# Two softmax attentions with heads in pairs on half the array each, and weights kept in rows padded with zeros

## The chip, the cores and the metric

The kernel runs on one core of one Trainium2 chip, in one launch. The metric is the device time of that launch in microseconds. A core has five engines that work beside each other and wait for one another by semaphores: PE (the 128x128 matrix array), DVE (vector), ACT (scalar), POOL, and SP, which here only issues DMAs. PE writes to PSUM; DVE and ACT empty it.

## The reference, cut to what matters

A model of three attention layers on 256 tokens with 16 more in front (272 keys): a mixer with two attentions (`stick_breaking`, and `dsa_attention`, a softmax over the keys that an index picks), a mixture of 32 experts, a retention layer, and an attention with latent keys and values (MLA), the second softmax. All in f32, width 1024. The parts that the change touches:

```
def dsa_attention(q_full, kv_all, q_idx, w_idx, k_idx, pos, topk):       # 8 heads, key width 16 + 128
        s_idx = relu(einsum('bqhd,bkd->bqhk', qi, k_idx))                 # index heads of width 64
        score = einsum('bqh,bqhk->bqk', wi, s_idx);  _, sel = top_k(masked score, topk)      # topk 64
        logits = einsum('bqhc,bqkc->bqhk', qf, kv_sel) * scale
        p = softmax(where(valid, logits, -1e30))
        return einsum('bqhk,bqkc->bqhc', p, kv_sel[..., ROPE_DIM:])
def mla_mixer(...):                                                       # 8 heads, key width 128 + 64
        sc = einsum('bqhd,bkhd->bhqk', q[:, s:e], k[:, :e])               # query blocks of 128
        p = softmax(where(mask, sc, MASK_VALUE));  outs.append(einsum('bhqk,bkhd->bqhd', p, v[:, :e]))
```

A query of the first block of 128 sees the keys 0 to 143 only, one of the second block all 272.

## The kernel before

Everything but the attentions is dense matmuls of streamed weights: `Stream.next` cuts a weight block into a high and a low part (L285 on ACT, L286 on DVE), `tiles` issues three matmuls for each 128x128 block (L298 to L300), moving 256 or 272 columns. `dense` makes one output tile of it, in two halves, and between them calls `step`, which advances every generator in `self.gens` by one `yield`. The attentions are such generators, so each of their steps stands in the middle of a dense tile on PE. A planner of the language then moves instructions of each engine somewhat against the order of the code, by its own costs. DMAs are all on the SP queue, in order.

The pieces that the change touches:

- `index` in `mixer` (L579 to L602): scores of 8 index heads of width 64 against one key head, for both query blocks (144 and 272 keys), one head per step; ReLU on ACT (L589), weighted sum on DVE (L591); then eight steps of top-k on DVE (L597, L598), which leave the mask `msk`.
- `latent` in `mixer` (L548 to L573): the keys `kf` and the values `vb` from the latent. The values of the keys 128 to 143 and 256 to 271 go as two 16-row pieces to rows 0 to 15 and 32 to 47 of the third block of `vb`.
- `sparse` in `mixer` (L697 to L721): the first softmax attention, ten steps. Step n issues the scores of head n (per query block: the mask added by a bf16 matmul, L718, and then a matmul over the 64 rows of the head, L719) and `weigh`; then `turned` of head n - 1; and, at odd heads, the `mix` of the two heads before.
- `weigh` (L1440): softmax of one head's 128 x 416 scores (two query blocks side by side, 144 + 272): two maxima and their scaling on DVE (L1448, L1449), two exponentials on ACT (L1451), the reciprocal and two scalings on DVE (L1452, L1454).
- `turned` (L1457): the weights transposed on PE: three 128x128 pieces (L1464 to L1466) and two of 16 rows (L1467; L1468, a plain matmul with the identity, in two passes), then copies (L1470 on ACT, L1473 and L1474 on DVE, to `rest`).
- `mix` (L1477): three matmuls per head (L1480 to L1482), the middle one over the 48 rows of `rest`.
- `turn` and `attention` in `latent` of the second model (L1373 to L1407): the same for the last attention, two heads per generator, key width 128 (L1393) plus 64 (L1394), and values transposed in two full and two 16-row pieces (L1379, L1380).

`stick`, the first layer's other attention, is untouched. It already takes its heads in pairs: the two heads' matmuls of 64 rows stand next to each other, one on rows 0 to 63 and one on rows 64 to 127 (L651), and its mix writes columns 0 to 63 and 64 to 127 (L685).

An f32 matmul is two passes (two weight loads and two matmuls) in the profile; transposes, bf16 and the dense f32r matmuls are one.

Behind the first mixer, the memory of its attentions is given back (`early.close()`), and the loads of expert weights into `raw2` (L1027, on SP) wait for that.

## Time and profile before

| | |
|---|---|
| median of 3 runs | 1544.19 us (1543.4 to 1546.91) |
| the profiled execution | 1543.42 us |
| its span, first to last instruction | 1541.6 us |
| mean granted clock of PE | 0.918 |
| PE busy | 1368.4 us (89%), 9784 instructions |
| PE weight loads | 1067.3 us (69%) |
| DVE busy | 738.2 us (48%) |
| ACT busy | 532.5 us (35%) |
| POOL busy | 131.8 us (9%) |

A shape such as 64*128 64x144 is the used part of the array (rows*columns) and the moving operand. In timelines an instruction's length is from its start to the end of its result, and neighbours on PE overlap; how much time one takes from PE is read from the next one's start. A row with x4 merges four instructions of one line.

### The profile page before, as it was taken

The numbers are of one execution on the slowest core, as the hardware profiler recorded it, in microseconds if no ns is written. First come the engines' busy times: TensorE is split into PE (matmuls) and PEld (weight loads), VectorE is DVE, ScalarE is ACT, GpSimd is POOL, SyncE is SP. The second block draws the span as 40 slices with busy tenths as digits, with TensorE's granted clock in tenths as the row PEclk, the third lists the DMA queues.
The fourth block names the chain that finished last, engine by engine and source line by source line (L and its number), as shares of the span: only waits on it lengthen the run. The fifth ranks groups of instructions, "written<-read, shape, count | busy, mean of one in ns | idle before, by whom it ended". The sixth has DMA issues, their size and how long they took to land.

```text
span 1541.6 us, 23923 instructions
## 1 busy us (share of the span) xinstructions
PE 1368.4 (89%) x9784; PEld 1067.3 (69%) x9784; DVE 738.2 (48%) x1464; ACT 532.5 (35%) x928; POOL 131.8 (9%) x146
## 2 busy tenths in 40 slices
PE   8999998776676767666999999999999999999997
PEld 7898796221111212113999999999999877899997
DVE  7676566110100101003766665766567755666654
ACT  5465443100000000004233443544445443454442
POOL 4010021000000000002121211100011201100001
PEclk9999998976868768777999999999999999999998
DMA  8433386999999999997434344455545423355551
GB/s 300 124 124 97 110 286 260 420 419 371 421 420 420 421 420 421 421 421 318 153 114 148 133 141 154 154 175 169 187 164 180 160 87 108 111 169 189 189 179 71
DMA packets 55267, 359.56 MB, mean 233 GB/s; under 512 B 6384, under 2 KB 7024, under 8 KB 15600
## 3 DMA queue, kind: packets, MB, share of 16 engines
q1 hardware_dynamic: 55152, 357.97, 61.5%
q8 instruction: 79, 1.29, 0.3%
q14 instruction: 36, 0.29, 0.1%
HBM read 356.90 MB, written 1.05 MB: 232 GB/s over the span
## 4 chain that ended last, share of the span: by engine, by line
PE 49%; DVE 2%; ACT 1%; issue 0%; POOL 0%; DVEq 0%; ACTq 0%; POOLq 0%
PE acc L298 14%; PE acc L300 14%; PE acc L299 14%; DVE wl L286 1%; PE att L383 1%; ACT wh L285 1%; PE att L1394 1%; PE att L414 1%; PE att L1295 0%; PE att L1271 0%; DVE U L290 0%; PE att L1393 0%; PE att L1297 0%; PE att L1285 0%; PE att L1296 0%
## 5 line engine op out<-in xcount | busy, mean ns | idle before, releaser
L298 PE MATMUL acc<-U,wh 128*128 128x272 f32 (+1 forms) x1456 | 426.1, 293 | 12.0 <-ACT U L289 7.0
L299 PE MATMUL acc<-U,wl 128*128 128x272 f32 (+1 forms) x1456 | 418.9, 288 | 2.0 <-DVE wl L286 2.0
L300 PE MATMUL acc<-U,wh 128*128 128x272 f32 (+1 forms) x1456 | 419.1, 288 | 0.0
L286 DVE TENSOR_TENSOR wl<-raw,wh 128x1024 fp32r<-128x1024 f32 x232 | 285.9, 1232 | 155.8 <-ACT wh L285 155.3
L285 ACT ACTIVATE wh<-raw 128x1024 fp32r<-128x1024 f32 x232 | 245.6, 1060 | 319.2 <-PE acc L300 214.0
L298 PEld LDWEIGHTS acc<-U,wh 128*128 128x128 f32 x1456 | 277.9, 191 | 20.7 <-issue 8.2
L299 PEld LDWEIGHTS acc<-U,wl 128*128 128x128 f32 x1456 | 277.1, 190 | 2.6 <-DVE wl L286 2.4
L300 PEld LDWEIGHTS acc<-U,wh 128*128 128x128 f32 x1456 | 276.9, 190 | 0.4
L974 PE MATMUL acc<-raw,U 128*32 128x512 f32 x1024 | 190.4, 837 | 91.1 <-DMA raw<-in_wm 87.1
L974 PEld LDWEIGHTS acc<-raw,U 128*32 128x32 f32 x1024 | 24.6, 125 | 240.3 <-DMA raw<-in_wm 216.4
L985 DVE TENSOR_TENSOR hid<-hid,acc 128x512 f32<-128x512 f32 x8 | 5.5, 688 | 262.5 <-PE acc L974 262.5
L300 PE MATMUL acc<-hl,wh 128*128 128x272 f32 (+1 forms) x352 | 100.1, 284 | 0.0
L299 PE MATMUL acc<-hh,wl 128*128 128x272 f32 (+1 forms) x352 | 99.8, 284 | 0.0
L298 PE MATMUL acc<-hh,wh 128*128 128x272 f32 (+1 forms) x352 | 99.8, 284 | 0.0
L286 DVE TENSOR_TENSOR wl<-rawh,wh 128x512 fp32r<-128x512 f32 x112 | 80.6, 731 | 26.5 <-ACT wh L285 26.4
L1000 PE MATMUL att<-raw,ht 128*32 128x512 f32 x512 | 73.6, 690 | 19.3 <-DMA raw<-in_wm 15.6
L285 ACT ACTIVATE wh<-rawh 128x512 fp32r<-128x512 f32 x112 | 68.1, 626 | 46.8 <-PE acc L300 33.1
L1009 DVE TENSOR_TENSOR h<-h,att 128x512 f32<-128x512 f32 x32 | 22.0, 688 | 118.4 <-PE att L1007 118.4
L298 PEld LDWEIGHTS acc<-hh,wh 128*128 128x128 f32 x352 | 66.4, 189 | 0.0
L300 PEld LDWEIGHTS acc<-hl,wh 128*128 128x128 f32 x352 | 66.2, 188 | 0.0
L299 PEld LDWEIGHTS acc<-hh,wl 128*128 128x128 f32 x352 | 66.0, 187 | 0.0
L373 POOL TENSOR_TENSOR s<-s,sq 128x256 f32<-128x256 f32 (+1 forms) x24 | 20.7, 880 | 498.5 <-ACT sq L369 498.0
(404 smaller groups left out, 1966.6 us busy)
## 6 DMA issues: line engine op xcount, KB each, us to landing
raw<-in_wm SPq DMA_DIRECT2D x192, 1024.0 KB, 19.8
raw<-in_ws SPq DMA_DIRECT2D x116, 1024.0 KB, 4.9
rawh<-in_ws SPq DMA_DIRECT2D x56, 512.0 KB, 3.9
const<-in_const SPq DMA_DIRECT2D x1, 1056.0 KB, 8.5
out<-Q SPq DMA_DIRECT2D x4, 256.0 KB, 2.5
h<-in_xt SPq DMA_DIRECT2D x2, 272.0 KB, 4.6
h<-in_xt SPq DMA_DIRECT2D x1, 544.0 KB, 7.8
small<-in_small SPq DMA_DIRECT2D x1, 512.0 KB, 5.9
```

Of the source, the lines that this page charges most:

```text
L285: self.nc.scalar.activation(hi, src, AF.Copy)
L286: self.nc.vector.tensor_sub(lo, src, hi.bitcast(F32))
L298: mm(p[:, :n], wh, xh[:, kb, c0:c0 + n], start=kb == first, stop=False)
L299: mm(p[:, :n], wl, xh[:, kb, c0:c0 + n], start=False, stop=False)
L300: mm(p[:, :n], wh, xl[:, kb, c0:c0 + n], start=False, stop=kb == nkb - 1)
L373: self.nc.gpsimd.tensor_add(s[0], s[0], t)
L383: self.nc.tensor.matmul(p[:m, k + i:k + i + 1], x[:, c:c + m], self.ones[:, 0:1], start=s is ss[0] and x is s[0] and i == 0, stop=True, sk ...
L414: self.nc.tensor.matmul(p[:, c:c + m], y[:m, i:i + 1].to_broadcast([m, P]), self.c("ident")[:m, :m], start=True, stop=True)
L974: mm(p[32 * e:32 * e + 32], XG[:, j % 2, kb, c:c + 32], w[:, 512 * e:512 * e + 512], start=kb == 0, stop=kb == KB - 1)
L1000: mm(p[32 * e:32 * e + 32], ht[:, f * P + e * 32:f * P + e * 32 + 32], w[:, 512 * e:512 * e + 512], start=f == 0, stop=f == 3)
L1009: dve.tensor_add(h[:, k:k + 2, NM:], h[:, k:k + 2, NM:], p.rearrange("p (j n) -> p j n", j=2))
L1394: mm(p[:, c:c + n], qr[o:o + 64, q0:q0 + P], kr[o:o + 64, :n], start=False, stop=True)
```

## The change

`index`, `sparse` and the last attention take two heads per step. The scores of head 2p stand on rows 0 to 63 of the array, those of head 2p + 1 on rows 64 to 127, next to each other and into two PSUM tiles. The mask of both query blocks (416 columns) is added by one matmul per head. The softmax weights live in tiles of 640 columns (`weights`), where each query block's row is padded with zeros to full 128-key pieces; the padding is written once. `turned` then transposes five 128x128 pieces, some of which are partly overwritten by the next, and copies 512 columns; `mix` has three matmuls, over 256, 192 and 64 queries, all with 128 keys. The latent `ckv` and the values `vt` of the last attention are padded with zeros in the same way, so that the third block of values is a full one. `rests`, `rest` and the 16-row pieces are gone. `sparse` has nine steps: the pair's scores, then `turned` of both, then the mix with the next pair's scores. In the last attention both heads' scores stand in one step.

```
-                for hd in range(8):
-                    b, o = hd // 2, 64 * (hd % 2)
+                for pair in range(4):
+                    p = [self.att() for _ in range(2)]
                     for i, n in cut:
-                        p = self.att()
-                        mm(p[:, :n], qi[o:o + 64, b, i * P:(i + 1) * P], ki[o:o + 64, :n], start=True, stop=True)
...
+                        for j in range(2):
+                            o = slice(64 * j, 64 * j + 64)
+                            mm(p[j][:, 144 * i:144 * i + n], qi[o, pair, i * P:(i + 1) * P], ki[o, :n], start=True, stop=True)
+                    for j in range(2):
+                        hd = 2 * pair + j
+                        rl = wa.tile([P, 416], F32, name="rl")
+                        act(rl, p[j][:, :416], AF.Relu)
...
-                for i in range(2):
+                for i in range(3):
                     p = self.att()
                     mm(p, ckv[:, i * P:(i + 1) * P], wuv, start=True, stop=True)
                     act(vb[:, i], p, AF.Copy)
...
+                def scores(pair):
+                    p = [self.att() for _ in range(2)]
+                    cut = ((0, 0, 144), (P, 144, T))
+                    for j in range(2):
+                        mm(p[j][:, :416], self.identb, msk, start=True, stop=True)
+                    for q0, c, n in cut:
+                        for j in range(2):
+                            o = slice(64 * j, 64 * j + 64)
+                            mm(p[j][:, c:c + n], qb[o, pair, q0:q0 + P], kf[o, pair, :n], start=False, stop=True,
+                               skip_group_check=True)
+                    ws_[pair] = [self.weigh(x, 0.125) for x in p]
+                def mixed(pair):
+                    py, t = self.att(), ts.pop(pair)
+                    for i in range(3):
+                        for j in range(2):
+                            o, hd = 64 * j, 2 * pair + j
+                            self.mix(py[o:o + 64], t[j], vb[:, i, hd * 64:hd * 64 + 64], i)
+                    self.split(ybh[:, pair], ybl[:, pair], py[:, :NX])
+                for step in range(9):
+                    if step % 2:
+                        ts[step // 2] = [self.turned(w) for w in ws_.pop(step // 2)]
+                    else:
+                        if step:
+                            mixed(step // 2 - 1)
+                        if step < 8:
+                            scores(step // 2)
                     yield
...
-                    for i, c, n in ((0, 0, P), (1, P, P), (2, P, 16)):
-                        nc.tensor.transpose(p[:n, i * P:(i + 1) * P], vt[:, c:c + n], ident)
-                    mm(p[32:48, 256:384], vt[:, 256:], ident, start=True, stop=True)
...
+                    for i in range(3):
+                        nc.tensor.transpose(p[:, i * P:(i + 1) * P], vt[:, i * P:(i + 1) * P], ident)
+                    act(v.rearrange("p a b -> p (a b)"), p[:, :3 * P], AF.Copy)
...
+                        mm(ps[j][:, :416], self.identb, msk, start=True, stop=True)
+                        for q0, c, n in cut:
+                            mm(ps[j][:, c:c + n], qn[j][:, q0:q0 + P], kn[j][:, :n], start=False, stop=True,
+                               skip_group_check=True)
+                    for q0, c, n in cut:
+                        for j in range(2):
+                            o = slice(64 * j, 64 * j + 64)
+                            mm(ps[j][:, c:c + n], qr[o, q0:q0 + P], kr[o, :n], start=False, stop=True,
+                               skip_group_check=True)
+                    ws_ = [self.weigh(p, 192 ** -0.5) for p in ps]
+                    yield
+                    yield
...
+    KEYS = ((0, 256, 0), (256, 448, 64), (448, 512, 192))
+    def weights(self, pool, n):
+        self.sw, self.nsw = [], 0
+        for i in range(n):
+            t = pool.tile([P, 5, P], F32, name=f"sm_w{i}").rearrange("p a b -> p (a b)")
+            self.nc.gpsimd.memset(t[:, 144:256], 0.0)
+            self.nc.gpsimd.memset(t[:, 528:640], 0.0)
+            self.sw.append(t)
...
+        pp, tr, id_ = self.att(), self.nc.tensor.transpose, self.c("ident")
+        for c, k in ((0, 0), (192, 128), (128, 256), (384, 512), (320, 384)):
+            tr(pp[:, c:c + P], w[:, k:k + P], id_)
+        pt = self.wa.tile([P, 512], F32, name="sm_t")
+        self.nc.scalar.activation(pt, pp, AF.Copy)
+        return pt
+    def mix(self, po, pt, val, i):
+        c0, c1, q0 = self.KEYS[i]
+        self.nc.tensor.matmul(po[:, q0:NX], val, pt[:, c0:c1], start=i == 0, stop=i == 2)
```

How it moves instructions, at three places. First PE in the middle of `sparse` before: behind 24 dense matmuls the mix of two heads (`vb` are the values, `sm_t` and `rest` the turned weights), then `turned` of the next head (`const0` is the identity).

```order
L1480 MATMUL att_1855<-sm_t_1737,vb_105 64x256
L1481 MATMUL att_1855<-rest0_98,vb_105 64x256
L1482 MATMUL att_1855<-sm_t_1737,vb_105 64x128
L1480 MATMUL att_1855<-sm_t_1799,vb_105 64x256
L1481 MATMUL att_1855<-rest1_100,vb_105 64x256
L1482 MATMUL att_1855<-sm_t_1799,vb_105 64x128
L1464 MATMUL att_1864<-const0_129,sm_w_1810 128x128
L1465 MATMUL att_1864<-const0_129,sm_w_1810 128x128
L1466 MATMUL att_1864<-const0_129,sm_w_1810 128x128
L1467 MATMUL att_1864<-const0_129,sm_w_1810 16x128
L1468 MATMUL att_1864<-const0_129,sm_w_1810 16x128
```

PE at the same place now: the mix of a pair with the two heads in turn, and directly behind it the next pair's masks and scores.

```order
L1487 MATMUL att_1768<-sm_t_1722,vb_105 64x256
L1487 MATMUL att_1768<-sm_t_1730,vb_105 64x256
L1487 MATMUL att_1768<-sm_t_1722,vb_105 64x192
L1487 MATMUL att_1768<-sm_t_1730,vb_105 64x192
L1487 MATMUL att_1768<-sm_t_1722,vb_105 64x64
L1487 MATMUL att_1768<-sm_t_1730,vb_105 64x64
L706 LDWEIGHTS identb_69
L706 MATMUL att_1777<-msk_108,identb_69 128x416
L706 LDWEIGHTS identb_69
L706 MATMUL att_1778<-msk_108,identb_69 128x416
L710 MATMUL att_1777<-kf_104,qb_106 128x144
L710 MATMUL att_1778<-kf_104,qb_106 128x144
```

Two L710 of 272 columns follow, then 24 dense matmuls, and then the ten transposes of both heads in a row, again 24 dense matmuls ahead of the next mix. Before, every 24 dense matmuls were followed by one head's transposes and one head's scores.

DVE beside one head's scores before: the maxima of `weigh` in `sparse` (`sm_m`), a product of the dense tile behind (L732), the sums' reciprocal and the scaling of the weights, then two splits of streamed weights.

```order
L1448 TENSOR_REDUCE sm_m_1879<-att_1874 128x1 x2
L1449 TENSOR_SCALAR sm_m_1879<-sm_m_1879 128x2
L732 TENSOR_TENSOR A_1399<-acc_1836,row_182 128x256
L1452 RECIPROCAL sm_s_1880<-sm_s_1880 128x2
L1454 TENSOR_SCALAR sm_w_1881<-sm_w_1881,sm_s_1880 128x144
L1454 TENSOR_SCALAR sm_w_1881<-sm_w_1881,sm_s_1880 128x272
L286 TENSOR_TENSOR wl_2044<-rawh_2041,wh_2043 128x512
```

DVE there now, for a pair:

```order
L1465 TENSOR_REDUCE sm_m_1785<-att_1777 128x1 x2
L1465 TENSOR_REDUCE sm_m_1795<-att_1778 128x1
L1466 TENSOR_SCALAR sm_m_1785<-sm_m_1785 128x2
L1465 TENSOR_REDUCE sm_m_1795<-att_1778 128x1
L1466 TENSOR_SCALAR sm_m_1795<-sm_m_1795 128x2
L741 TENSOR_TENSOR A_1372<-acc_1749,row_181 128x256
L1469 RECIPROCAL sm_s_1786<-sm_s_1786 128x2
L1471 TENSOR_SCALAR sm_w0_98<-sm_w0_98,sm_s_1786 128x144
L1471 TENSOR_SCALAR sm_w0_98<-sm_w0_98,sm_s_1786 128x272
L1469 RECIPROCAL sm_s_1796<-sm_s_1796 128x2
L1471 TENSOR_SCALAR sm_w1_101<-sm_w1_101,sm_s_1796 128x144
L1471 TENSOR_SCALAR sm_w1_101<-sm_w1_101,sm_s_1796 128x272
```

The second head's maxima stand between the first head's, its scaling behind the first head's, and the splits of weights behind both.

PE in the last attention, scores of one head before (`kr` and `qr` are the 64 rotary rows); 12 dense matmuls follow and then the second head's.

```order
L1392 LDWEIGHTS identb_69
L1392 MATMUL att_11268<-constb_10550,identb_69 128x144
L1393 MATMUL att_11268<-kn0_11044,qn0_11151 128x144
L1394 MATMUL att_11268<-kr_10714,qr_11212 128x144
L1392 LDWEIGHTS identb_69
L1392 MATMUL att_11268<-constb_10550,identb_69 128x272
L1393 MATMUL att_11268<-kn0_11044,qn0_11151 128x272
L1394 MATMUL att_11268<-kr_10714,qr_11212 128x272
```

PE there now, both heads:

```order
L1395 LDWEIGHTS identb_69
L1395 MATMUL att_11207<-constb_10491,identb_69 128x416
L1397 MATMUL att_11207<-kn0_10988,qn0_11093 128x144
L1397 MATMUL att_11207<-kn0_10988,qn0_11093 128x272
L1395 LDWEIGHTS identb_69
L1395 MATMUL att_11208<-constb_10491,identb_69 128x416
L1397 MATMUL att_11208<-kn1_11044,qn1_11118 128x144
L1397 MATMUL att_11208<-kn1_11044,qn1_11118 128x272
L1402 MATMUL att_11207<-kr_10658,qr_11150 128x144
L1402 MATMUL att_11208<-kr_10658,qr_11150 128x144
L1402 MATMUL att_11207<-kr_10658,qr_11150 128x272
L1402 MATMUL att_11208<-kr_10658,qr_11150 128x272
```

The matmuls on the full array come first for both heads, those of 64 rows last, in pairs. 24 to 36 dense matmuls stand between them and the first head's transposes, and 15 to 18 (10 in the first block) between those and the second head's.

## Rows read from the trace of the kernel before

**Rows 1.** Sums by stretch: us, busy time (count) of each engine, PEclk, DMA share, GB/s

```profile
37.00:187.00 150.00, 149.79 (x1069) 122.67 (x1069) 95.78 (x246) 82.84 (x179) 8.40 (x10) 1.00 0.34 106
270.00:720.00 450.00, 315.19 (x1779) 85.95 (x1779) 44.11 (x110) 32.46 (x61) 4.53 (x6) 0.76 1.00 416
1222.00:1313.00 91.00, 90.91 (x607) 72.39 (x606) 48.54 (x113) 38.26 (x89) 7.55 (x8) 1.00 0.31 105
```

**Rows 2.** Waits of the SP queue at L1027, expert weights: total us, times, longest

```profile
SPq L1027 <- DVE A L290: 11.5, 1, 11.5
...
SPq L1027 <- PE att L1482: 2.1, 1, 2.1
```

**Rows 3.** Timeline of PE, one index head: start us, us, engine, line, what

```profile
49.61 0.28 PE L299 MATMUL acc<-U,wl 128*128 128x272 f32 x1
49.73 0.29 PE L300 MATMUL acc<-U,wh 128*128 128x272 f32 x1
49.95 0.97 PE L587 MATMUL att<-ki,qi 64*128 64x144 f32 x4
50.85 0.39 PE L298 MATMUL acc<-U,wh 128*128 128x272 f32 x1
```

**Rows 4.** Timeline of PE, a pair of stick: masks, scores, and its mix later

```profile
108.94 0.51 PE L647 MATMUL att<-constb,identb 128*128 128x416 bf16 x2
109.38 1.07 PE L651 MATMUL att<-qa,ka 64*128 64x256 f32 x12
...
113.43 0.97 PE L685 MATMUL att<-sb_w,B 128*64 128x256 f32 x12
```

**Rows 5.** Timeline of PE, sparse: mix of two heads, turned and scores of one

```profile
145.50 0.65 PE L1480 MATMUL att<-sm_t,vb 128*64 128x256 f32 x2
...
148.17 0.33 PE L1464 MATMUL att<-const,sm_w 128*128 128x128 f32 x1
...
153.52 0.27 PE L1464 MATMUL att<-const,sm_w 128*128 128x128 f32 x1
...
155.85 0.38 PE L298 MATMUL acc<-U,wh 128*128 128x256 f32 x1
```

**Rows 6.** Timeline of PE, last attention: scores of one head

```profile
1254.96 0.24 PE L1392 MATMUL att<-constb,identb 128*128 128x144 bf16 x1
...
1255.99 0.62 PE L1393 MATMUL att<-kn,qn 128*128 128x272 f32 x2
1256.54 0.72 PE L1394 MATMUL att<-kr,qr 64*128 64x272 f32 x2
1257.20 0.39 PE L298 MATMUL acc<-ckh,wh 128*128 128x272 f32 x1
```

**Rows 7.** Timeline of PE, last attention: turned of one head, turn of one head's values

```profile
1241.23 0.27 PE L1464 MATMUL att<-const,sm_w 128*128 128x128 f32 x1
...
1242.08 0.39 PE L298 MATMUL acc<-cqh,wh 128*128 128x256 f32 x1
...
1262.64 0.49 PE L1379 MATMUL att<-const,vt 128*128 128x128 f32 x3
...
1263.38 0.40 PE L298 MATMUL acc<-ckh,wh 128*128 128x272 f32 x1
```

**Rows 8.** Timeline of PE, last attention: mix of one head

```profile
1272.31 0.59 PE L1480 MATMUL att<-sm_t,vb 128*128 128x256 f32 x2
...
1273.71 0.37 PE L298 MATMUL acc<-cqh,wh 128*128 128x256 f32 x1
```

**Rows 9.** Timelines of DVE and of ACT, softmax of one head of sparse

```profile
150.66 0.66 DVE L1448 TENSOR_REDUCE sm_m<-att 128x1 f32<-128x144 f32 x2 [0.32 <-PE att L719]
...
152.82 0.57 DVE L1454 TENSOR_SCALAR sm_w<-sm_w,sm_s 128x144 f32<-128x144 f32 x2
...
151.56 0.38 ACT L1451 ACTIVATE sm_w<-att,sm_m 128x144 f32<-128x144 f32 x1 [1.82 <-DVE sm_m L1449]
...
152.39 0.63 ACT L285 ACTIVATE wh<-rawh 128x512 fp32r<-128x512 f32 x1
```

More of the change, by code (lines that the diff above doesn't have):

```diff
@@ L481, in mixer @@
             kw = m.tile([P, T], F32, name="kw")
[L482 removed]
+            ckv = m.tile([P, 3 * P], F32, name="ckv")
             self.consts(m, "small1", False)
@@ L486, in mixer @@
             cr, sr, sbm = self.c("c1"), self.c("s1"), self.c("sbmask")
-            self.rests(m)
+            self.weights(m, 2)
             kf = m.tile([P, 4, T], F32, name="kf")
@@ L491, in mixer @@
             wi = m.tile([P, 16], F32, name="wi")
-            msk = [m.tile([P, T], BF16, name=f"msk{i}") for i in range(2)]
+            msk = m.tile([P, 416], BF16, name="msk")
             self.nones = m.tile([P, P], F32R, name="nones")
@@ L1404, in attention @@
                         po = self.att()
-                        self.mix(po, ts[j], lambda t, k: vb[j][k, t])
+                        for i in range(3):
+                            self.mix(po, ts[j], vb[j][:, i], i)
                         self.split(yh[:, 2 * b + j], yl[:, 2 * b + j], po[:, :NX])
@@ L1414, in latent @@
                         kn.append(k)
-                        vt = w.tile([P, T], F32, name="vt")
-                        dve.tensor_mul(vt, self.dense(ws, 4, ckh, ckl), rk)
+                        vt = w.tile([P, 3 * P], F32, name="vt")
+                        gps.memset(vt[:, T:], 0.0)
+                        dve.tensor_mul(vt[:, :T], self.dense(ws, 4, ckh, ckl), rk)
                         v = w.tile([P, 3, P], F32, name=f"vb{j}")
@@ L1444, in weigh @@
         sm = wa.tile([P, 2], F32, name="sm_s", bufs=4)
-        w = wa.tile([P, 416], F32, name="sm_w")
-        cut = ((0, 0, 144), (1, 144, 416))
-        for i, a, b in cut:
-            dve.tensor_reduce(mx[:, i:i + 1], p[:, a:b], axis=AX.X, op=ALU.max)
+        w = self.sw[self.nsw % len(self.sw)]
+        self.nsw += 1
+        cut = ((0, slice(0, 144), slice(0, 144)), (1, slice(144, 416), slice(256, 528)))
+        for i, a, _ in cut:
+            dve.tensor_reduce(mx[:, i:i + 1], p[:, a], axis=AX.X, op=ALU.max)
@@ L1455, in weigh @@
         return w
     def turned(self, w):
-        nc, wa = self.nc, self.wa
-        pp = self.att()
-        id_ = self.c("ident")
-        tr = nc.tensor.transpose
-        tr(pp[:, 0:128], w[:, 0:128], id_)
-        tr(pp[:, 128:256], w[:, 144:272], id_)
-        tr(pp[:, 256:384], w[:, 272:400], id_)
-        tr(pp[:16, 384:512], w[:, 128:144], id_)
-        nc.tensor.matmul(pp[32:48, 384:512], w[:, 400:416], id_, start=True, stop=True)
-        pt = wa.tile([P, 384], F32, name="sm_t")
-        nc.scalar.activation(pt, pp[:, :384], AF.Copy)
@@ L1484, in attend @@
-    def attend(self, po, p, scale, val):
-        self.mix(po, self.turned(self.weigh(p, scale)), val)
+        pp, tr, id_ = self.att(), self.nc.tensor.transpose, self.c("ident")
[7 more added lines that the diff above has]
+        self.nc.tensor.matmul(po[:, q0:NX], val, pt[:, c0:c1], start=i == 0, stop=i == 2)
```

89 lines of the change are left out of this document (17 added, 72 removed).

## Prediction

> **What bounds the kernel now.** I read the sums by stretch first [rows 1]. In the two stretches that hold the edited code, 37 to 187 us (first attention layer) and 1222 to 1313 us (last one), PE has no idle time (149.79 of 150 us, 90.91 of 91) at the full granted clock, 1.00, which is 2.4 GHz, while DVE, ACT and the DMA engines are busy 64%, 55% and 34% or less. So in both stretches time on PE is time on the path. Between them lies the expert layer, 270 to 720 us, where the DMA engines are full (1.00, 416 GB/s) and PE is not. Whether a gain of the first stretch survives it depends on what starts that stream. The SP queue says it [rows 2]: its first blocked expert load waits for the last `mix` of the first attention (L1482, 2.1 us), and the longest wait (11.5 us) is for DVE's tile A at L290, the last arithmetic before the routing. Both are program events behind the attention. The stream starts when they come, so it moves with them, and its own length does not change. The last stretch is followed by work bound by PE, so its gain goes to the end directly.
>
> The timeline is then read by starts. Matmuls are pipelined: one lasts 0.28 us, but the dense ones start 0.12 us apart (49.61, 49.73 in [rows 3]). The price of a group is the distance from its first start to the next dense start, plus 0.10 where that dense matmul lasts 0.39 instead of 0.29, plus 0.10 at the entry (49.73 to 49.95 is 0.22, not 0.12). These two tenths come wherever the used part of the array changes from the full 128x128 to 64 or 48 rows or to 64 or 16 columns, or back.
>
> **The change part by part.** Index scores. One head costs 0.90 + 0.10 + 0.10 = 1.10 us for 4 passes (each f32 matmul is two passes) of together 832 columns [rows 3], eight times. What a pair on two halves of the array costs is in the trace already, since `stick` does it: 12 passes, for two heads of 832 columns each, last 1.07 us, where the 4 passes of one head last 0.97 [rows 3, 4]. So the second head rides along, and four groups of 1.10 go: **4.4 us**.
>
> First softmax attention (`sparse`), per pair of heads, before: two `mix` 2.67 us (145.50 to 148.17) + 0.10 for the entry; twice `turned` and scores, 153.52 to 155.85 with the tenth behind it, 2.43 each [rows 5]. Sum 2.77 + 4.86 = 7.63. After: the mix is six matmuls like L685 of `stick`, whose 12 passes last 0.97, or 0.90 to the next start (groups of this kind last 0.07 longer than they hold PE [rows 3]). It gets 1024 columns per head (2 x 512) for 832, and a column of an f32 pass takes 0.84 ns: 1255.99 to 1256.54 holds two passes of 272 and one change of shape, (0.55 - 0.10)/2 = 0.23 us each [rows 6]. So 0.90 + 0.16 + 0.10 = 1.16. Scores: both masks with the entry 0.44 (108.94 to 109.38), the paired group 1.00, the tenth behind it: 1.54 [rows 4]. `turned`: ten transposes on the full array. Three last 0.49 and one 0.27, so they start 0.11 apart [rows 7]: 1.10. Sum 3.80; saved 3.83 x 4 = **15.3 us**.
>
> Last attention, per pair, before: scores 1254.96 to 1257.20, 2.34 a head [rows 6]; `turned` 0.95 and `turn` of the values 0.84 [rows 7]; `mix` 1.40 + 0.08 = 1.48 [rows 8]. Two of each: 11.22. After: masks 0.34, the `qn` part on the full array 1664 columns x 0.84 = 1.40, the `qr` part paired like an index group 1.10, ten transposes 1.10, six for the values 0.66. The mix is 0.86 a head by columns; its two passes of 64 columns would last 0.05 each, but loads of 128 weight columns follow one another at 0.11 at best (the transposes' spacing), so I take 0.97, 1.94 for both. Sum 6.54; saved 4.68 x 4 = **18.7 us**. The third piece of the latent's values, which becomes full, I cost at nothing: 512 columns take the same passes with 16 rows in use or 128.
>
> New waits. The order shows that `turned` of both heads now stands 24 dense matmuls after the scores, as it stood for one head. For one head the chain on DVE and ACT runs from 150.66 (maximum) to 152.82 + 0.57 = 153.39 (weights scaled), and PE comes for it at 153.52 [rows 5, 9]: 0.13 us to spare. With two heads the DVE order has the second head's maxima inside the first head's chain and its scaling behind. The second head trails by at least ACT's 0.83 for one head's exponentials (151.56 to 152.39), so it is ready at about 154.2 to 154.4, while its transposes are due 0.55 after the first head's, at 154.07. I take 0.2 us of waiting per pair, since only the later transposes need the last scaled piece: 0.8 in `sparse`. In the last attention the second head's transposes stand 15 dense matmuls further on, some 1.8 us, and hide it; 0.3 for the first heads. On DVE the next splits of weights (L286) are queued behind the waiting scaling; PE has weights split several groups ahead and didn't wait for them in either stretch [rows 1], so that costs nothing while it lasts under some 2 us. What leaves DVE and ACT (two copies of the remainder per head, small copies of the values) and comes to POOL (filling zeros) lies beside PE: nothing either way.
>
> One step moves: the top-k follows the index scores four tiles earlier and leaves the stretch where `stick` starts. Its DVE work is the same, so nothing. `sparse` ends one dense tile earlier in PE's order, so the 2.1 us for which the SP queue was blocked [rows 2] go; this lets weights arrive earlier in front of the expert layer, worth 0 to 2.1, and I take 0.7.
>
> Sum: 4.4 + 15.3 + 18.7 = 38.4, less 1.1 of waits, plus 0.7: **38.0 us**. Against the profiled execution (span 1541.6, 1543.42 with 1.8 around it) that is 1505.4; it lies 0.8 under the median of 1544.19, which becomes **1506.2**.
>
> A row that could be read against the ten transposes: one lasts 0.27 us [rows 7], and the change has 80 where 64 and 16 two-pass matmuls stood. What the engine loses is the 0.11 between starts. The Trainium skill, TensorE: Matmul & The Clock Gate, Part 4 (PE-mode transpose), gives about 275 ns for one in a kernel's context. As a duration this trace agrees (0.27); taken as the price of each it would make the rival below.
>
> **Rivals.** (a) The softmax chain ends last: the two heads' chains run one after the other. Each is 2.73 long, the second is ready at 156.1 and due at 154.07, so 2.0 us per pair, 8.2 in `sparse`, 7.4 more than I took: 1514. For it: DVE works strictly in the order given, and head one has only 0.13 us to spare [rows 9]. Against it: the interleaved order. The Trainium skill, TensorEngine Tiling (Array Packing), section Performance Considerations, warns of just this, that array packing speeds up TensorE but not the emptying of PSUM; no row of before shows two softmax heads at once.
>
> (b) The halves don't run side by side in the new places, so the change doesn't do what it says. Each paired group pays its second head: 0.70 for 832 columns in 12 groups (index, scores, `qr`), 0.86 in 4 mixes, 11.8 us: 1518. Against it: two groups of the same shapes do it in `stick` [rows 4].
>
> (c) The expert stream doesn't start earlier and swallows the first stretch's 19 us: 1525. For it: 416 GB/s for 450 us. Against it: [rows 2].
>
> (d) Each transpose holds the array for its recorded 0.27 us: `turned` at 1.35 instead of 0.55 in 16 places, the values at 0.81 instead of 0.33 in 8: 16.6 us less gained, 1523. Against it: the starts 0.11 apart.
>
> (e) Slower than before: the clock. Where PE had holes it fell (0.76 in the expert layer [rows 1]). If the waits of (a) let the granted clock fall to 1.2 GHz and it stayed there through `sparse`, the four pairs with their eight dense tiles of 24 matmuls 0.12 apart, 4 x 3.8 + 8 x 2.9 = 38 us, would take twice that: 38 + 8 lost against 38 gained, 1552. It decides from some four fifths of that stretch at half clock. Against it: waits of 2 us four times in 46 are far fewer holes than the expert layer's 135 us idle in 450.
>
> **How the numbers follow.** Forecast 0.85; (a) 0.06, (b) 0.03, (c) 0.02, (d) 0.01, (e) 0.02; 0.01 for several of (b) to (d) together, which would end within 0.2%. The forecast's own spread is the sum's rounding (two tenths at some 100 changes of shape, +-2), waits of 0 to 5 and the 0 to 2.1 of the stream: 1501 to 1512; up to (a), 1515. By over 0.2% (about 3 us, what a measurement of this kernel can tell from no change): faster 0.97, same 0.01, slower 0.02.
>
> **What would show it.** The index rows should appear four times with next dense starts about 0.9 later; each paired group as pairs of matmuls starting within hundredths of a microsecond; five transposes 0.11 apart. PE should still be full in the first stretch, now some 20 us shorter; the expert stream should start about 20 us earlier and last as long; the last attention should take about 72 us for 91. Wrong would be: waits of PE for DVE at the transposes of over 0.5 us (a), a group of a pair of 1.7 us (b), an expert layer that ends where it did (c), a clock under 1.00 between 130 and 170 us (e).

## The result

| | before | after |
|---|---|---|
| median on record | 1543.8 us (4 runs, 1541.9 to 1546.91) | 1500.48 us (4 runs) |
| the profiled execution and its span | 1543.42, 1541.6 us | 1498.93, 1497.1 us |
| PE busy, mean granted clock | 1368.4 us, 0.918 | 1314.9 us, 0.931 |
| the same two kernels again, on one chip, 9 and 5 runs | 1541.25 us (1538.33 to 1544.38) | 1502.69 us (1498.73 to 1505.49) |

The ratio is 0.9719 (95% interval 0.97 to 0.9739), and 0.9738 (0.9721 to 0.9755) the second time: faster by 43 and by 39 us, where 38.0 was forecast. The median on record lies 0.5 us under the range of 1501 to 1515. (It is the middle of 1495.94, 1498.93 and 1502.03 and of one execution of 2085.73 at a mean granted clock of 0.55, which the ratio leaves out.)

The sums by stretch of the changed kernel, to set beside [rows 1] (the third window ends earlier in the program than the one of before): us, busy time (count) of PE, PEld, DVE, ACT and POOL, PEclk, DMA share, GB/s.

```profile
37.20:167.20 130.00, 129.67 (x1053) 116.85 (x1053) 89.75 (x230) 81.79 (x170) 8.41 (x10) 1.00 0.39 119
247.50:697.30 449.80, 305.81 (x1785) 83.45 (x1783) 45.80 (x112) 33.88 (x65) 4.91 (x7) 0.81 1.00 416
1199.10:1270.90 71.80, 71.77 (x554) 67.01 (x553) 42.18 (x92) 33.33 (x66) 8.71 (x14) 1.00 0.36 120
```

The first stretch is 20 us shorter and PE still has no idle time in it. The expert layer begins 22.5 us earlier, and from the last dense matmul in front of it to the first one behind it are 469.9 us for 472.6, at 416 GB/s in both. From the dense matmul at 1198 us of before to the one behind the last attention's last mix are 108.1 us for 126.5, 18.4 us less. All three are as forecast.

A ledger is made from the 6912 dense matmuls, which are the same in both kernels: it says how much earlier the same matmul starts. What a stretch gains is the difference of two such numbers. Two of its points, before and then the changed kernel, are the dense matmul behind sparse and the one behind the last mix:

```profile
186.85 0.39 PE L298 MATMUL acc<-U,wh 128*128 128x256 f32 x1
...
1324.39 0.37 PE L298 MATMUL acc<-yh,wh 128*128 128x256 f32 x1
```

```profile
166.99 0.28 PE L298 MATMUL acc<-U,wh 128*128 128x256 f32 x1
...
1283.38 0.36 PE L298 MATMUL acc<-yh,wh 128*128 128x256 f32 x1
```

The column "second trace" has the gains in another execution of the changed kernel (`after_again`, below).

| stretch, by the clock of before | earlier at its end, us | gained in it | second trace | forecast |
|---|---|---|---|---|
| start, to 57 us | -0.24 | -0.2 | -4.0 | 0 |
| index, to 77 | 4.11 | 4.35 | 4.35 | 4.4 |
| `stick`, to 128 | 4.07 | 0.0 | 0.0 | 0 |
| sparse, to 187 | 19.96 | 15.9 | 15.9 | 15.3 - 0.8 of waits |
| up to the expert layer, 248 | 22.51 | 2.6 | 1.1 | 0.7 |
| experts to the last attention, 1198 | 22.64 | 0.1 | -0.4 | 0 |
| last attention and what follows, to 1357 | 42.18 | 19.5 | 18.6 | 18.7 - 0.3 of waits |
| last down-projection, to 1528 | 44.52 | 2.3 | 2.3 | 0 |
| sum | | 44.5 | 37.9 | 38.0 |

Up to the last mix, at 1324, the last attention gains 18.4 in the first trace and 18.6 in the second. The other 1.2 us of the first lie behind it and are not the change's: PE waits there 2.6 to 2.7 us for DVE, and then before goes on at a granted clock of 0.50 and the first trace of the changed kernel at 1.00. The second trace goes on at 0.50 as before does. About the same piece of the program in before, the first and the second trace of the changed kernel:

```profile
1337.50:1340.00 2.50, 2.50 (x14) 2.50 (x14) 2.29 (x4) 2.50 (x6) 1.85 (x3) 0.50 0.00 0
```

```profile
1296.30:1298.80 2.50, 2.48 (x22) 2.27 (x20) 2.50 (x4) 2.50 (x6) 2.09 (x3) 1.00 0.02 7
```

```profile
1301.50:1304.00 2.50, 2.50 (x14) 2.50 (x14) 2.13 (x3) 2.50 (x7) 2.16 (x3) 0.50 0.08 30
```

PE in a pair of sparse, the timeline of the changed kernel: start us, us, engine, line, what. It answers to [rows 4, 5]; the dense matmuls at 131.56, 141.04 and 146.44 mark the ends of groups, and the first pair's transposes stand in front.

```profile
130.49 1.31 PE L1479 MATMUL att<-const,sm_w 128*128 128x128 f32 x10
131.56 0.37 PE L298 MATMUL acc<-U,wh 128*128 128x256 f32 x1
...
139.92 1.36 PE L1479 MATMUL att<-const,sm_w 128*128 128x128 f32 x10
141.04 0.36 PE L298 MATMUL acc<-U,wh 128*128 128x256 f32 x1
...
144.06 1.09 PE L1487 MATMUL att<-sm_t,vb 128*64 128x256 f32 x12
145.08 0.53 PE L706 MATMUL att<-msk,identb 128*128 128x416 bf16 x2
145.53 0.97 PE L710 MATMUL att<-kf,qb 64*128 64x144 f32 x8
146.44 0.39 PE L298 MATMUL acc<-U,wh 128*128 128x256 f32 x1
```

Mix 1.02 + 0.10 (1.16 was forecast), masks and scores 1.36 + 0.10 (1.54), ten transposes 1.12 (1.10 and 0.2 of waiting). The first pair's transposes, which don't wait, take 1.07; so the second head's wait 0.05.

Why they hardly wait is seen on DVE and ACT, the same pair (it answers to [rows 9]).

```profile
137.06 0.87 DVE L1465 TENSOR_REDUCE sm_m<-att 128x1 f32<-128x144 f32 x3 [0.51 <-PE att L710]
...
139.28 0.57 DVE L1471 TENSOR_SCALAR sm_w<-sm_w,sm_s 128x144 f32<-128x144 f32 x2
139.91 0.17 DVE L1469 RECIPROCAL sm_s<-sm_s 128x2 f32<-128x2 f32 x1
140.11 0.57 DVE L1471 TENSOR_SCALAR sm_w<-sm_w,sm_s 128x144 f32<-128x144 f32 x2
...
138.10 0.38 ACT L1468 ACTIVATE sm_w<-att,sm_m 128x144 f32<-128x144 f32 x1 [2.00 <-DVE sm_m L1466]
...
138.94 0.38 ACT L1468 ACTIVATE sm_w<-att,sm_m 128x144 f32<-128x144 f32 x1
```

The first head's weights are scaled at 139.85 and its transposes begin at 139.92; the second head's are scaled at 140.68, 0.83 later, which is what its exponentials trail (138.94 for 138.10). Its last transposes need them only then.

PE in a pair of the last attention, scores (they answer to [rows 6]):

```profile
1227.07 0.35 PE L1395 MATMUL att<-constb,identb 128*128 128x416 bf16 x1
1227.26 0.87 PE L1397 MATMUL att<-kn,qn 128*128 128x144 f32 x4
1227.96 0.34 PE L1395 MATMUL att<-constb,identb 128*128 128x416 bf16 x1
1228.14 0.87 PE L1397 MATMUL att<-kn,qn 128*128 128x144 f32 x4
1228.94 0.97 PE L1402 MATMUL att<-kr,qr 64*128 64x144 f32 x8
1229.84 0.39 PE L298 MATMUL acc<-ckh,wh 128*128 128x272 f32 x1
```

2.77 + 0.10 for both heads, where 2.84 was forecast and one head took 2.34 before.

### The profile page after: what moved, and what is told of

Its sections match the earlier page's. It is cut to its first block, busy times and chain, and to the rows that moved or that the text cites. A ratio compares the mean times of both kernels' runs of the same rounds, so it can differ in the third digit from the quotient of the medians.

```text
span 1497.1 us, 23804 instructions
## 1 busy us (share of the span) xinstructions
PE 1314.9 (88%) x9734; PEld 1051.7 (70%) x9734; DVE 724.4 (48%) x1417; ACT 528.3 (35%) x903; POOL 134.3 (9%) x165
## 4 chain that ended last, share of the span: by engine, by line
PE 47%; DVE 2%; ACT 1%; issue 0%; POOL 0%; DVEq 0%; ACTq 0%; POOLq 0%
PE acc L298 14%; PE acc L300 14%; PE acc L299 14%; DVE wl L286 1%; ACT wh L285 1%; PE att L414 0%; PE att L1487 0%; PE att L1304 0%; PE att L1280 0%; PE att L383 0%; DVE U L290 0%; PE att L1306 0%; PE att L1397 0%; PE att L1294 0%; PE att L1305 0%
## 5 line engine op out<-in xcount | busy, mean ns | idle before, releaser
L298 PEld LDWEIGHTS acc<-U,wh 128*128 128x128 f32 x1456 | 276.6, 190 | 17.6 <-ACT U L289 7.4
L983 PE MATMUL acc<-raw,U 128*32 128x512 f32 x1024 | 186.2, 820 | 91.0 <-DMA raw<-in_wm 87.3
L1009 PE MATMUL att<-raw,ht 128*32 128x512 f32 x512 | 68.6, 635 | 28.7 <-DMA raw<-in_wm 25.1
```

Of the source, the lines that this page charges most:

```text
L298: mm(p[:, :n], wh, xh[:, kb, c0:c0 + n], start=kb == first, stop=False)
L983: mm(p[32 * e:32 * e + 32], XG[:, j % 2, kb, c:c + 32], w[:, 512 * e:512 * e + 512], start=kb == 0, stop=kb == KB - 1)
L1009: mm(p[32 * e:32 * e + 32], ht[:, f * P + e * 32:f * P + e * 32 + 32], w[:, 512 * e:512 * e + 512], start=f == 0, stop=f == 3)
```

## Experiments

**One half of the change at a time.** `mixer_only` has the first layer as changed and the last attention as before, `mla_only` the other way round. The core of the edit in `mixer_only`, against the changed kernel:

```
-            msk = self.grp["constb"][:, 416:832]
-            self.weights(m, 3)
+            msk = [self.c("cm0"), self.c("cm1")]
+            self.rests(m)
...
-                    ws_ = [self.weigh(p, 192 ** -0.5) for p in ps]
+                        ws_.append(self.weigh1(p, 192 ** -0.5))
```

> The first layer's index, latent and sparse as in the changed kernel, the last attention as before (its tiles too, so that the down-projection's moving operand hh lies at byte 138752 of a partition as before, and not at 136448 as in the changed kernel). Theory (each stretch keeps its own gain, the expert stream starts with the attention's end): index 4.3 and sparse 15.9 as in the trace of the changed kernel, the expert stream starts about 22 us earlier and is as long as before, the last attention takes its 91 us: about 22 us less than before, 1521. Rival (the expert stream swallows what is gained ahead of it): it ends where it did, within 3 us of before. Of the down-projection at the end, whose matmuls start 0.113 apart in the changed kernel and 0.118 before: 0.118 here if the place of hh in memory sets it, 0.113 if anything in the first layer does.

> The last attention as in the changed kernel, the first layer as before; hh lies at byte 136448 as in the changed kernel. Theory: the last attention takes 19.5 us less, as in the trace of the changed kernel, and the down-projection's matmuls start 0.113 apart (2.3 us less over 528 of them): about 22 us less than before, 1521; the two halves of the change add up to what both do together. Rival (the down-projection's pitch is an accident of one execution): 0.118 there, 1524. Rival (a gain is lost to a wait behind the attention): a new wait of PE in the stretch that follows the last attention, and less than 15 us in all.

Measured: 1520.21 us, ratio 0.9874 (0.984 to 0.9908), and 1524.8 us, 0.9886 (0.9846 to 0.9926). By the ledger `mixer_only` gains 4.35 in index, 15.9 in sparse and 21.0 up to the experts, and keeps it through them (it holds 25.6 at the end; some 3 of the further 4.6 come directly behind the expert layer, where before runs two stretches at half clock). `mla_only` gains 18.4 in the last attention. So the halves add up, 21.0 and 18.4 to 39 us (22.1 and 17.5 by the medians, where the whole change has 38.6), and the expert stream swallows nothing: rival (c) falls. The down-projection's matmuls start 0.118 apart in both, also in `mla_only`, where the operand lies where it does in the changed kernel. Its 2.3 us belong to neither half as an edit.

**Scores in pairs without the padding.** The changed order of steps and the paired scores, with `turned`, `mix` and the values as before:

```
-        for c, k in ((0, 0), (192, 128), (128, 256), (384, 512), (320, 384)):
-            tr(pp[:, c:c + P], w[:, k:k + P], id_)
+        tr(pp[:, 0:128], w[:, 0:128], id_)
+        tr(pp[:, 128:256], w[:, 144:272], id_)
+        tr(pp[:, 256:384], w[:, 272:400], id_)
+        tr(pp[:16, 384:512], w[:, 128:144], id_)
+        nc.tensor.matmul(pp[32:48, 384:512], w[:, 400:416], id_, start=True, stop=True)
```

> Only the scores are taken in pairs (index, sparse, last attention, with one mask of 416 columns a head); the weights stay in rows of 416 columns, and the transposes (three full pieces, two of 16 rows), the 48-row middle matmul of the mix and the values are as before. Worked out from the traces of before and of the changed kernel: index 4.3; sparse's scores of a pair 1.46 against 2 x 1.48, four times 1.5 = 6.0; the last attention's 2.86 against 4.68, four times 1.8 = 7.3; together 17.6 us less than before, 1524 beside 1542. The rest of the change's 44 (about 22 in the two attentions) is then due to the padding. Rival (the padding only follows from the pairs and brings nothing by itself): over 35 us less. Rival (with both heads' weights in a row the narrow pieces wait for their copies): a wait of PE for the copies to the 48-row tile in front of each mix, and less than 12 us gained.

Measured: 1523.8 us, ratio 0.9872 (0.985 to 0.9894). By the ledger index 4.35, sparse 6.5 and the last attention 6.8, together 17.6 as expected; no wait of PE for the narrow copies in either attention. The padding and what goes with it bring the rest: 9.4 in sparse and 11.6 in the last attention, 21 us. In sparse this holds the mix with its heads in turn, too, which this run has head by head; the next run puts 2 us on that order.

**Are the halves side by side, and must they be neighbours?** First the order alone: all of one head, then all of the other.

```
-                    for q0, c, n in cut:
-                        for j in range(2):
+                    for j in range(2):
+                        for q0, c, n in cut:
                             o = slice(64 * j, 64 * j + 64)
                             mm(p[j][:, c:c + n], qb[o, pair, q0:q0 + P], kf[o, pair, :n], start=False, stop=True,
                                skip_group_check=True)
```

> The changed kernel with the same matmuls in another order: all of head 2p first and then all of head 2p + 1, so that no matmul of one half of the array has one of the other half next to it, but for the middle of a group. Theory (the halves run side by side only as neighbours, and that is what the pairs bring): each of 12 groups of scores pays its second head, 0.70 us, and each of 4 mixes 0.86, together 11.8 us: 1511 against 1499; in the timeline a group of scores lasts 1.67 instead of 0.97. Rival (the gain comes from fewer, full pieces and fewer changes of shape): no difference, 1499, groups of 0.97. Since the one place in the middle of a group has neighbours on two halves, one pass of each can still overlap: then a tenth to a fifth less than 11.8.

Measured: 1503.26 us, ratio 0.9758 (0.9725 to 0.9792), beside 0.9738 for the changed kernel. Both theories missed. The timeline of PE in a pair of sparse:

```profile
134.51 1.57 PE L1487 MATMUL att<-sm_t,vb 128*64 128x256 f32 x12
136.02 0.53 PE L706 MATMUL att<-msk,identb 128*128 128x416 bf16 x2
136.47 0.98 PE L710 MATMUL att<-kf,qb 64*128 64x144 f32 x8
```

The scores still last 0.98: the second head's first matmul starts 0.014 after the first head's first, although the code puts two matmuls, four passes, of the first head before it. (The trace does not hold the order in which the planner left them. That it kept the code's is argued from the distance, which is 0.007 in the changed kernel, where one matmul stands ahead, and from the mix, which did get longer.) So an order by heads doesn't take the overlap of row halves away. The mix on column halves does lose: 1.57 instead of 1.09, 0.5 us in each pair, 2 us in all. The run did not do what it was made for, so the next one puts both heads on the same rows, with every instruction in its place:

```
-                            mm(p[j][:, c:c + n], qb[o, pair, q0:q0 + P], kf[o, pair, :n], start=False, stop=True,
+                            mm(p[j][:, c:c + n], qb[:64, pair, q0:q0 + P], kf[:64, pair, :n], start=False, stop=True,
                                skip_group_check=True)
```

> The changed kernel with both heads of a pair on rows 0 to 63 in the three groups of scores (index, sparse, the qr part of the last attention), and every instruction in the same place; so the second heads compute with the first heads' rows, and the output isn't the reference's. In the run with the heads one after the other the halves still ran beside each other (their matmuls start 0.01 apart in an order that isn't the code's), so that run did not take the overlap away; this one does. Theory: of a group of 8 passes the second head's four follow the first's, 0.70 us more in each of 12 groups, 8.4 us in all: 1507 against 1499, a group lasts 1.67 instead of 0.97 in the timeline. Rival (the gain is from fewer changes of shape and fuller pieces): groups of 0.97, the same time.

Measured: 1510.34 us, ratio 0.981 (0.9793 to 0.9826). The same place in the timeline:

```profile
139.58 1.67 PE L710 MATMUL att<-kf,qb 64*128 64x144 f32 x8
141.18 0.39 PE L298 MATMUL acc<-U,wh 128*128 128x256 f32 x1
```

1.67 for 0.97, the 0.70 that rival (b) put on it from [rows 3]. By the ledger the four groups of the index cost 2.8 us, those of sparse 2.4 and those of the last attention 2.5: 7.7 in all, where 8.4 were priced. In the changed kernel the halves do run side by side, and that is worth a fifth of its gain.

**Two chains in a row.** One buffer for the maxima, so that the second head's chain starts when the first's exponentials are done:

```
-        mx = wa.tile([P, 2], F32, name="sm_m", bufs=4)
+        mx = wa.tile([P, 2], F32, name="sm_m", bufs=1)
+        wa.tile([P, 24], F32, name="sm_p", bufs=1)
```

> The changed kernel with one buffer for the softmax maxima instead of four (the memory is kept, so nothing else moves): the second head's maxima can't be written before the first head's exponentials have read theirs, and the two chains run one after the other, which was rival (a). Theory (the order of DVE, which interleaves the chains, is what keeps the second head's transposes from waiting; in the changed kernel they wait 0.08 us a pair): the second head is ready 1.4 to 2 us later, and PE waits that much in front of its five transposes in each of the four pairs of sparse, 5 to 8 us in all; nothing in the last attention, where the second head's transposes come 15 dense matmuls later. Rival (there is slack of a microsecond or two that the rows don't show): no wait, the same time. The other rival: the wait lets the granted clock fall, and the stretch takes more than the sum of the waits.

Measured: 1508.17 us, one run. The timeline of PE in the second pair of sparse, and then, from the waits of PE and of the SP queue, one row each:

```profile
140.62 0.71 PE L1480 MATMUL att<-const,sm_w 128*128 128x128 f32 x5
141.08 0.37 PE L298 MATMUL acc<-U,wh 128*128 128x256 f32 x1
...
143.05 0.41 PE L1480 MATMUL att<-const,sm_w 128*128 128x128 f32 x2 [0.30 <-DVE sm_w L1472]
143.21 0.37 PE L298 MATMUL acc<-U,wh 128*128 128x256 f32 x1
143.42 0.49 PE L1480 MATMUL att<-const,sm_w 128*128 128x128 f32 x3
```

```profile
PE acc L298 <- DVE h L781: 3.1, 1, 3.1
...
SPq L1036 <- PE att L1488: 4.5, 1, 4.5
```

The chain is as long as rival (a) had it, but PE waits 0.3. The planner put the second head's transposes 12 dense matmuls later (and two of them ahead of the last scaling). A pair loses 0.5 us (2.0 in sparse by the ledger), not 2. The larger loss is an indirect one: the last mix comes later, the SP queue is blocked 4.5 us for it, and PE waits 3.1 us in front of the expert layer, a stretch that loses 3.8 in all against the changed kernel's first trace. That weights come late by the blocked queue is read from these waits, no run changes it alone. The other 3.4 of the 9.3 us lie mostly in stretches of half clock, below.

**What does an execution by itself bring?** The changed kernel once more, beside the others.

> The changed kernel once more, beside the others on the same chip. Theory (the down-projection's rhythm and the stretches of half clock are decided anew in each execution, not by the program): the two attentions take the same as in the first trace within 0.2 us, while the down-projection's matmuls may start 0.113 or 0.118 apart (2.3 us) and the number of 3 us stretches at half clock may differ (1.5 us each): 1499 to 1504. Rival (they belong to the program): the same trace everywhere.

Measured: 1502.69 us, spans of the two traces 1497.1 and 1503.7. From index to sparse's end the two agree within 0.1 us, and in the last attention, up to its last mix, within 0.3. The difference is elsewhere: dense matmuls that last 0.43 instead of 0.28, in stretches of about 3 us behind holes of PE, at a granted clock of 0.50 (1.2 GHz). The same piece of the program in the changed kernel's first trace and then before's:

```profile
953.00:954.50 1.50, 1.50 (x8) 1.50 (x8) 1.01 (x7) 0.88 (x1) 0.00 (x0) 0.50 0.04 11
```

```profile
977.00:978.50 1.50, 1.50 (x13) 1.50 (x13) 1.20 (x8) 0.92 (x1) 0.00 (x0) 1.00 0.00 0
```

PE had the same hole in front in both (it waits 1.0 us for POOL), and one execution went on at half clock and the other didn't. Before has 4 such stretches (14.5 us), the changed kernel 3 (11.5 us) and the second time 8 (23.7 us); half of their length is lost. That is 6 of the 6.6 us between the changed kernel's two traces.

**The pace of the dense matmuls.** In 65 us of the down-projection, changed kernel and then `apart`, whose program is the same there:

```profile
1417.00:1482.00 65.00, 65.00 (x572) 65.00 (x572) 35.53 (x42) 29.81 (x41) 7.14 (x6) 1.00 0.43 147
```

```profile
1421.00:1486.00 65.00, 65.00 (x553) 65.00 (x552) 34.02 (x41) 28.98 (x39) 7.13 (x6) 1.00 0.42 146
```

572 matmuls, 0.1136 apart, against 553, 0.1175 apart. A kernel of its own measures the pace of dense matmuls with nothing else running:

```
        for n, row, a, b, m in segments():
            p = ps.tile([P, 512], F32, name="acc")
            mm(p[:, :m], wh[:, :P], xh[:, :m], start=True, stop=True)
            for k in range(16):
                c, d = a // 4 + k % 8 * (row // 4), b // 4 + k % 8 * P
                mm(p[:, :n], wh[:, d:d + P], xh[:, c:c + n], start=k == 0, stop=False)
                mm(p[:, :n], wl[:, d:d + P], xh[:, c:c + n], start=False, stop=False)
                mm(p[:, :n], wh[:, d:d + P], xl[:, c:c + n], start=False, stop=k == 15)
```

> Not the reference's work at all: 153 series of 48 dense f32r matmuls (weights high, low, high as the kernels have them), in which nothing else runs, with the moving operand's and the weights' place in memory shifted by steps of 32 or 64 bytes, and 26 series with the same places behind a matmul of 32 to 232 columns. In the down-projection the same matmuls with the same places started 0.113 apart in two runs (the changed kernel, serial) and 0.118 in two others (mla_only, apart). Theory (the rhythm in which weight loads and matmuls alternate is set by what ran ahead, and then holds): the 26 series with one place fall into two or more rhythms, 0.113 and 0.118 among them. Rival (place alone): they are all alike, and the shifted ones differ. Second rival (traffic of the other engines): all series at one place and of one width are alike, at about 0.113.

None of the theories held as it stood. All 26 series at one place keep 117.8 ns, whatever ran ahead. Place does matter, but neither of the two addresses by itself: the pace goes by their difference, moving operand minus weights, modulo 256 bytes (256 columns, rows 1024 bytes apart; mean distance of starts in the second half of each series, worked out from the trace):

```
difference mod 256, bytes     0     32     64     96    128    160    192    224
mean of the series, ns    120.0  116.8  117.8  120.0  118.7  118.2  113.8  118.4
lowest, ns                120.0  116.6  117.7  119.8  118.5  117.4  113.3  118.2
highest, ns               120.0  117.8  117.8  120.2  118.8  118.9  117.8  118.5
```

At 192 nine of ten series keep 113.3 and one 117.8. The kernels' 256-column tiles of U with rows of 1024 bytes lie at 96 and keep 120.0 there too. The down-projection lies at 64 in all kernels but `placed`, and in nine traces it has both paces: 113.3 in both traces of the changed kernel and in `serial`, 117.8 in the six others. The six dense matmuls in front of it, whose distances repeat in a cycle of six, stand at one and the same point of that cycle in those three and at other points in those six. That the point of entry decides is what these traces fit, no more.

**A version with operands placed by that table**, instruction for instruction the changed kernel:

```
+    def wide(self):
+        t = self.glob.tile([P, 2 * KB * T], F32R, name="U")
+        return t[:, 24:24 + 2 * KB * NX].rearrange("p (a k n) -> p a k n", a=2, k=KB)
...
-                u = self.glob.tile([P, 2, KB, NX], F32R, name="U")
+                u = self.wide()
...
+                if nb == 6:
+                    m.tile([P, 16], F32, name="cp")
...
+            q.tile([P, 32], F32, name="hp")
```

> The changed kernel, instruction for instruction, with moving operands at other places: the 256-column tiles of U 96 bytes higher, hh and hl 128, the last attention's cqh, cql, yh and yl 64, so that moving operand minus weights is 192 mod 256 bytes. In the run that had dense matmuls alone the spacing of starts went by that difference: 113.3 ns at 192, 117.8 at 64, 118.6 at 128, 120.0 at 0 and 96. Theory (the same holds in the kernel): 1248 matmuls of U at 113.3 for 120.0 (8.4 us), 528 of the down-projection at 113.3 for 117.8 or already there (0 to 2.4), 408 of the last attention at 113.3 for 118.6 (2.0): 10 to 13 us less than the changed kernel beside it, 1488 to 1491. Rival (in the kernel the other engines' traffic or the weights' arrival sets the pace): the spacing stays, no difference. Rival (the stretches are held by the weight stream's DMA or by its splits on DVE and ACT): the spacing falls and new waits of PE for the splits give half of it back.

Measured: 1496.91 us (1493.7 to 1499.06), ratio 0.9708 (0.969 to 0.9727), beside 1502.69 us and 0.9738 for the changed kernel: 5.8 us less by the medians, half of what was expected; the two intervals just overlap. In 110 us of the last gate and up projections, changed kernel and then this one:

```profile
1305.00:1415.00 110.00, 109.95 (x917) 109.77 (x916) 69.74 (x99) 53.81 (x79) 0.00 (x0) 1.00 0.53 182
```

```profile
1305.00:1415.00 110.00, 109.87 (x968) 109.70 (x967) 74.29 (x109) 56.29 (x82) 0.00 (x0) 1.00 0.56 192
```

968 for 917 matmuls in the same time: the pace fell from 0.120 to 0.1136, which over the 1056 of that stretch makes 6.7 us. The last attention's tiles came from 118.5 to about 115 and 116, not to 113.3, about 1 us. The 192 in front of the expert layer gained nothing, and the down-projection had nothing left to gain (113.3 in both). What of the difference between medians is half clock was not separated.

## Where the prediction was right, and which step failed

- **What bounds the kernel** was right: time on PE was time on the path in both stretches, and the expert stream moved as a whole [rows 1, 2]. **Prices** were right: an index pair, a group of scores (0.70 for a second head that doesn't ride along), transposes 0.109 apart, 4.68 for a pair of the last attention (the same matmuls of two successive pairs start 27.36 and 32.04 earlier). Rivals (b), (c) and (d) fall with the runs above; (e) too, since both stretches kept a clock of 1.00. Up to its last mix the last attention gained 18.4 and 18.6, where 18.4 was forecast.
- **The step that failed is the last, how the range follows from the numbers.** Its spread was the rounding of the sum, waits of 0 to 5 and up to 2.1 of the stream, and so it ended 5 us below the forecast. It put at nothing what one execution differs from the next by, though the three times of before spread over 3.5 us. The eight executions of the changed kernel that the two ratios use lie between 1495.94 and 1505.49, five of them in the range, with 1502.1 in the middle. The stretches of half clock (6 us between two traces) and the down-projection's two paces (2.3 us) are wider together than those 5 us. Of the 6.5 us that the first trace gained over the sum, 2.3 are the down-projection, 1.2 the half clock that before has behind the last attention and this trace has not, 1.9 the stretch up to the expert layer and 1.4 sparse (the points that follow). Before's median of 1544.19 was itself high: three later sets of seven to nine runs have 1540.64 to 1542.29.
- **That the second comparison comes out at 39 us is partly luck.** The second trace gained 38.9 in index, sparse and the last attention, where 37.3 was forecast, and 2.3 in the down-projection, which was put at nothing; 4.0 were lost ahead of 57 us, most of it in a stretch of half clock (17 to 25 us at 0.57, in the first trace at 1.00).
- **Waits were mis-sized**, 1.1 us taken and 0.2 found: 0.2 a pair in sparse were 0.05, and no wait for the softmax shows in the last attention, where 0.3 were taken. The interleaved order on DVE kept the second head 0.83 behind the first, and its transposes' last pieces are due about then. Rival (a) had the wrong price too: it held PE's order fixed. When the chains are made to run one after the other, the planner moves the transposes, and a pair loses 0.5.
- **The group of scores was priced a tenth too high** in sparse. The 1.00 is what 12 passes of `stick` take to the next dense start [rows 4]; the changed kernel's group has 8 and takes 0.91, as one head's four do [rows 3]. With the masks, the entry and the tenth behind it the sum is 1.46, not 1.54, and with the mix's 0.04 that is 0.5 us in four pairs. Against it stands a tenth that was left out: behind the ten transposes the first dense matmul lasts 0.36 and the next one starts 0.21 later instead of 0.12, though the used part stays 128x128, some 0.3 us in four pairs.
- **The freed SP queue was worth 0.4 to 1.2, where 0.7 was taken.** The wait that went with it stands in the waits of PE before, and is gone from the changed kernel:

```profile
PE acc L298 <- DVE h L772: 1.2, 1, 1.2
```

  Blocked 2.1 us, PE waited 1.2 in before and 0.4 in `mla_only`; not blocked, 0 to 0.2 (`placed`); blocked 4.5 us in `serial`, 3.1. The rest of the 2.6 us in that stretch is not shown to be the change's: waits for `rp_t`, 1.3 us before, are 0.7 and 1.4 in two executions of the changed kernel, and with the first layer as changed the stretch gained 2.6, 1.1, 0.8 (`mixer_only`) and 1.0 (`apart`), while `mla_only`, whose program is there the one of before, lost 1.2.
- Of the rule on transposes that was weighed (the Trainium skill, TensorE: Matmul & The Clock Gate, Part 4, about 275 ns each): behind ten of them the next dense matmul starts 1.07 us after the first one's start, so 275 ns is the duration of one (0.27 in [rows 7]) and not its price. Of the rule for rival (a) (the Trainium skill, TensorEngine Tiling (Array Packing), Performance Considerations, that PSUM's emptying may become the bottleneck): it did not here, PE waits 0.05 us a pair.

## What to carry to other kernels

Price a group of matmuls from its first start to the next dense start; prices read that way from a trace of before held to within about a tenth of a microsecond in kernels that put the groups elsewhere. Bringing narrow pieces (16 and 48 rows) up to full ones, with what goes with it, brought more here, 21 us, than putting two heads' scores on two halves of the array, 7.7. Put the executions' own spread into a range before the sum's, and place a moving operand by its distance to the weights.

## What the runs showed of the hardware

- Two matmuls on rows 0 to 63 and 64 to 127 need not be neighbours in the code: with two matmuls, four passes, of one half ahead, the other half's first still started 0.014 us after the first (`apart`; that the planner kept this order is argued, not seen). On column halves the order did matter (1.57 against 1.09). With both heads on one half of the rows a group took 1.67 for 0.97.
- The pace of dense f32r matmuls goes by the distance of moving operand and weights modulo 256 bytes: 113.3 to 120.0 ns for 256 columns. With rows of 1280 bytes and 272 columns it was 123.3 at 192 and 125.2 to 126.7 at 0, 64 and 128; with rows of 1088, 125.1 to 126.3.
- The same program behind the same hole went on at a granted clock of 1.00 or of 0.50. Behind the wait of 2.7 us that follows the last attention, two of ten traces (the changed kernel's first and `apart`) went on at 1.00, and eight ran some 3 us at 0.50. The changed kernel had 3 such stretches in one execution and 8 in another.
